# Last two feature blocks of the down projection with tokens stationary, and the final norm over rows

## The chip, the cores and the metric

The kernel runs on one core of one Trainium2 chip. The metric is the device time of one execution in microseconds (us). Five engines matter here: TensorE with its matmuls (PE in the profile) and its weight loads (PEld, a row of its own), VectorE (DVE), ScalarE (ACT), GpSimd (POOL) and the sync engine (SP), whose queue issues the DMAs. A matmul multiplies a stationary operand of 128 x up to 128, which a weight load brings in first, with a moving operand of 128 x N, and adds the product to an accumulator bank (PSUM) of 512 fp32 columns.

## The reference

One inference step of a two-layer decoder trunk over 256 prompt tokens and 64 sample tokens (T = 320 in all), D = 1024 features, fp32. Each layer is a mixer (spatial gating in layer 0, mLSTM in layer 1) and a gated MLP; every sub-layer has an RMS norm ahead and a residual add behind. What matters here is the end of the second layer:

```python
def conv_ffn(x, buf, w_up, conv_w, conv_b, w_down):
    up = x @ w_up
    a, g = jnp.split(up, 2, axis=-1)
    a_c, new_buf = causal_dwconv(a, buf, conv_w, conv_b)
    y = (jax.nn.gelu(a_c) * g) @ w_down
    return y, new_buf
...
x = x + y
return (rmsnorm(x, final_norm_g), ...)
# rmsnorm: x * rsqrt(mean(x*x over 1024 features) + EPS) * g
```

`w_down` is 2816 x 1024: 22 blocks of 128 on the contracted side (`KF`) and 8 blocks of 128 on the feature side (`KD`).

## The kernel before, in words

**Layout.** The activations are kept transposed: `xT[:, m, :]` holds feature block m (128 features on partitions) of all 320 tokens. Weights are stationary, tokens move. For fp32 accuracy each operand is split into a high part (`wh`, `yh`) and a low part (`wl`, `yl`), and each product is three matmuls: wh by yh, wh by yl, wl by yh (`chunk`, line 154). So one feature block of the last down projection is 22 x 3 = 66 matmuls of 128 x 320, accumulated in one bank `pm`.

**Weights.** `weights` (line 63) writes the list of all weight chunks in the order of their use; a chunk is up to 8 blocks of 128 x 128 (512 KB). `prefetch` (line 109) loads chunk i + 4 into one of four `raw` buffers through SP, and splits chunk i + 1 (`AHEAD`, `SPLIT_AHEAD`): ScalarE casts the high part (line 136), VectorE subtracts to get the low part (line 137), into one of three buffers. A down block is three chunks, of 8, 7 and 7 blocks. `take` (line 146) hands out the next chunk.

**Order.** The matmuls are pinned to the order of the program; a scheduler places the other engines' instructions.

**The end.** `ffn(1, None)` (line 448) makes 22 blocks of the gated hidden layer (`conv`, `gate`) and calls `final` (line 514). There, for each of the 8 feature blocks m: 66 matmuls into `pm`; three transposes of the block before into row banks `pyt` (tokens on partitions; `to_rows`, line 519); VectorE adds `pm` to `xT` (line 272); ScalarE squares the sum (line 192), and VectorE adds the squares up in `acc` (line 194); ScalarE multiplies by the norm vector, one value per partition (`xg`, line 536). After block 7: six matmuls against a matrix of ones sum the squares over the partitions (line 543), three transposes bring the last block into rows, VectorE turns the sums into means (line 545), GpSimd raises them to -1/2 (line 547), and ScalarE and VectorE scale one half each of the rows of three token tiles (two of 128 tokens, one of 64; lines 551, 552), which SP writes out, 512, 512 and 256 KB (line 553).

Of the kernel before, what the change touches and what calls it, by code (L numbers as in the profile page):

```python
# [16 lines left out]
P = 128  # L17
EPS = 1e-6
TINY = 1e-37
TP = 256  # L20
# [18 lines left out]
class Net:  # L39
# [23 lines left out]
    def weights(self):  # L63
# [42 lines left out]
    AHEAD, SPLIT_AHEAD = 4, 1  # L106
    EARLY_OUT = {(4, 5): (0, 1), (5, 3): (2,), (5, 5): (3, 4), (6, 3): (5,), (6, 5): (6, 7)}

    def prefetch(self, n, m):

        nc = self.nc
        while len(self.loaded) < min(n, len(self.wq)):
            w, b, k0, kn = self.wq[len(self.loaded)]
            raw = self.wraw.tile([P, 8, P], F32, tag="raw", name="raw")
            if w is self.I["a_wv"]:
                kn *= 4
                nc.sync.dma_start(raw[:, :kn, :], w[b, :, 4 * k0:4 * k0 + kn, :])
            else:
                nc.sync.dma_start(raw[:, :kn, :], w[b, :, k0:k0 + kn, :])
            self.loaded.append(raw)  # L120
        while len(self.halved) < min(m, len(self.wq)):
            i = len(self.halved)
            raw, kn = self.loaded[i], self.wq[i][3]
            if self.wq[i][0] is self.I["a_wv"]:
                kn *= 4
# [12 lines left out]
            self.halved.append((wh, wl))  # L138
# [45 lines left out]
    def square_block(self, m, keep=False):  # L184
# [5 lines left out]
        else:  # L190
            self.sq = self.tp.tile([P, T], F32, tag="sq", name="sq", bufs=2)
            nc.scalar.activation(self.sq, x, AF.Square)
            if not keep:
                nc.vector.tensor_tensor(self.acc, self.acc, self.sq, op=ADD)
# [253 lines left out]
    def ffn(self, l, gnext):  # L448
# [3 lines left out]
        with tc.tile_pool(name=f"yf{l}", bufs=1) as yp, tc.tile_pool(name=f"lf{l}", bufs=1) as lp:  # L452
            yh = yp.tile([P, KF, T], F32R, name=f"yh_f{l}")
# [31 lines left out]
            def gate(b, ps):  # L485
# [4 lines left out]
                self.split(yh[:, b, :], yl[:, b, :], y)  # L490
# [16 lines left out]
            rhs = lambda k: (yh[:, k, :], yl[:, k, :])  # L507
# [3 lines left out]
            else:  # L511
                self.final(lambda m: self.block(KF, rhs), lp)

    def final(self, block, lp):

        nc, O = self.nc, self.O
        pts = {}

        def to_rows(m, xg):
# [5 lines left out]
            for t in range(3):  # L525
                self.tr(pts[q][t][:, c * P:(c + 1) * P], self.tokens(xg, t), self.ident)

        prev = None
# [8 lines left out]
        pc = self.psm.tile([P, 512], F32, tag="pm", name="pc")  # L537
        pv = pc[:, 0:6].rearrange("p (t e) -> p t e", e=2)
        rc = self.tp.tile([P, 3], F32, tag="rc", name="rcf", bufs=2)
        ms = self.tp.tile([P, 3], F32, tag="ms", name="msf", bufs=2)  # L540
# [4 lines left out]
        nc.vector.tensor_scalar(ms, pv[:, :, 0], 1.0 / D, EPS, op0=MULT, op1=ADD)  # L545
        for t in range(3):
            nc.gpsimd.tensor_tensor(rc[:, t:t + 1], ms[:, t:t + 1], self.mhalf, op=ALU.pow)
        for t in range(3):
            ps, n = (slice(0, P), P) if t < 2 else (slice(64, P), 64)
            y = lp.tile([P, D], F32, tag="yo", name="yo", bufs=3)  # L550
            nc.scalar.activation(y[ps, 512:], pts[1][t][ps], AF.Copy, scale=rc[ps, t:t + 1])
            nc.vector.tensor_scalar(y[ps, :512], pts[0][t][ps], rc[ps, t:t + 1], None, op0=MULT)
            nc.sync.dma_start(O["y"][t * P:t * P + n, :], y[ps])
# [513 lines left out]
def _lay_out(i):  # L1067
# [20 lines left out]
    a["f_dn"] = np.stack([_blocks(i["f_w_down"][l]) for l in range(2)])  # L1088
    a["f_state"] = np.ascontiguousarray(i["state_ffn_conv"].reshape(2, 16, KF, P).transpose(0, 3, 2, 1))
# [73 lines left out]
```

## Time and profile before

| | us |
|---|---|
| three runs, median (lowest to highest) | 964.74 (964.19 to 965.17) |
| the profiled execution, its own time | 964.48 |
| its span, from the first to the last instruction | 962.8 |
| PE busy in the span | 948.8 |
| start of the last matmul of feature block 7 | 952.65 |

The profiled execution is 1.7 us longer than its span, and 0.26 us below the median of the runs. In the rows of a timeline the first column is the start in us from the span's start and the second the duration in us; then come engine, line, operation, written tile <- read tiles, shapes, and the count. In rows of the stage table the columns are the stretch, its length, the busy time of PE, PEld, DVE, ACT and POOL (with the count of instructions), the granted clock of PE as a share, the share of the DMA engines' time in use, and GB/s. In rows that group instructions, the two numbers after the bar are the busy time in us and the mean of one in ns, then the idle time before them.

### The profile page before, as it was taken

Reading aid. Unit: us, or ns where it says so; the run is one execution under the profiler, and the core shown is the slowest. Engines: PE = TensorE matmul, PEld = TensorE weight load, DVE = VectorE, ACT = ScalarE, POOL = GpSimd, SP = SyncE. Lnnn points to the kernel's source line nnn. Section 1 sums busy time; section 2 is a strip of 40 time slices with the busy share of each in tenths; the row PEclk is TensorE's granted clock in tenths of the full one; section 3 lists DMA queues with packets and bytes.
Section 4 is the critical chain, followed back from the end, with each engine's and each line's share of the span. In section 5 each row is a group of like instructions: output and inputs, shape, how many; then the busy total and the mean of one; then the engine's idle time right before and its main releaser. Section 6 shows DMA issues by size and latency. Waiting matters only on the chain.

```text
span 962.8 us, 17155 instructions
## 1 busy us (share of the span) xinstructions
PE 948.8 (99%) x6529; PEld 923.7 (96%) x6529; DVE 672.1 (70%) x1229; ACT 520.4 (54%) x948; POOL 79.5 (8%) x251
## 2 busy tenths in 40 slices
PE   9999999999999999999999999999999999999996
PEld 7779999999999999999899999999999999999996
DVE  5758985577777764549888877676787777775442
ACT  6557444355544543347777776575665555444332
POOL 2200000010000000013211001010101000000000
PEclk9999999999999999999999999999999999999998
DMA  7836344444444454456566555634473444445531
GB/s 252 237 131 183 125 139 150 148 142 154 153 141 152 145 153 151 148 196 209 192 203 203 178 174 187 209 127 152 87 247 136 154 154 150 139 147 153 155 121 55
DMA packets 57560, 154.71 MB, mean 161 GB/s; under 512 B 7734, under 2 KB 19382, under 8 KB 57478
## 3 DMA queue, kind: packets, MB, share of 16 engines
q1 hardware_dynamic: 57478, 153.62, 49.2%
q8 instruction: 51, 0.84, 0.3%
q14 instruction: 31, 0.25, 0.1%
HBM read 141.66 MB, written 11.94 MB: 160 GB/s over the span
## 4 chain that ended last, share of the span: by engine, by line
PE 85%; issue 10%; DVE 2%; DMA 1%; ACT 0%; SPq 0%; POOL 0%; DVEq 0%; POOLq 0%; ACTq 0%
PE pm L48 74%; PE pv L48 3%; PE num L48 2%; DMA raw<-in_a_wv 1%; PE pvs L48 1%; PE pmix L48 1%; DVE wl L137 1%; PE pCp L48 1%; PE psc L48 1%; PE pcs L48 1%; PE pv L51 1%; PE phn L51 0%; PE pk L51 0%; PE pc L48 0%; PE pg L48 0%
## 5 line engine op out<-in xcount | busy, mean ns | idle before, releaser
L136 ACT CAST wh<-raw 128x1024 fp32r<-128x1024 f32 (+3 forms) x255 | 257.9, 1012 | 306.5 <-PE pm L48 167.1
L137 DVE TENSOR_TENSOR wl<-raw,wh 128x1024 fp32r<-128x1024 f32 (+3 forms) x255 | 301.2, 1181 | 137.8 <-ACT wh L136 135.0
L48 PE MATMUL pm<-xh,wh 128*128 128x320 f32 x1216 | 379.7, 312 | 0.0
L48 PE MATMUL pm<-xh,wl 128*128 128x320 f32 x1216 | 376.0, 309 | 0.0
L48 PE MATMUL pm<-xl,wh 128*128 128x320 f32 x1216 | 375.8, 309 | 0.0
L48 PEld LDWEIGHTS pm<-xh,wh 128*128 128x128 f32 x1216 | 228.5, 188 | 0.7
L48 PEld LDWEIGHTS pm<-xl,wh 128*128 128x128 f32 x1216 | 228.5, 188 | 0.2
L48 PEld LDWEIGHTS pm<-xh,wl 128*128 128x128 f32 x1216 | 228.3, 188 | 0.0
L48 PE MATMUL pm<-yh_f,wh 128*128 128x320 f32 x352 | 109.2, 310 | 0.0
L48 PE MATMUL pm<-yh_f,wl 128*128 128x320 f32 x352 | 108.7, 309 | 0.0
L48 PE MATMUL pm<-yl_f,wh 128*128 128x320 f32 x352 | 108.7, 309 | 0.0
L48 PEld LDWEIGHTS pm<-yl_f,wh 128*128 128x128 f32 x352 | 66.1, 188 | 0.0
L48 PEld LDWEIGHTS pm<-yh_f,wh 128*128 128x128 f32 x352 | 66.1, 188 | 0.0
L48 PEld LDWEIGHTS pm<-yh_f,wl 128*128 128x128 f32 x352 | 66.1, 188 | 0.0
L478 DVE SCALAR_TENSOR_TENSOR fcv<-fpad,vecs,fcv 128x336 f32<-128x336 f32 x88 | 49.5, 565 | 2.2 <-ACT fcv L476 0.7
L272 DVE TENSOR_TENSOR xT<-pm,xT 128x320 f32<-128x320 f32 x40 | 19.6, 490 | 42.8 <-PE pm L48 42.8
L48 PE MATMUL pm<-yhb,wh 128*128 128x320 f32 x128 | 40.2, 314 | 0.0
L48 PE MATMUL pm<-yhb,wl 128*128 128x320 f32 x128 | 39.5, 309 | 0.5 <-DVE wl L137 0.5
L48 PE MATMUL pm<-yh_a,wh 128*128 128x320 f32 x128 | 39.6, 309 | 0.0
L48 PE MATMUL pm<-yl_a,wh 128*128 128x320 f32 x128 | 39.5, 309 | 0.0
L48 PE MATMUL pm<-yh_a,wl 128*128 128x320 f32 x128 | 39.5, 309 | 0.0
L48 PE MATMUL pm<-ylb,wh 128*128 128x320 f32 x128 | 39.5, 309 | 0.0
(254 smaller groups left out, 1273.7 us busy)
## 6 DMA issues: line engine op xcount, KB each, us to landing
raw<-in_f_up SPq DMA_DIRECT2D x88, 512.0 KB, 3.3
raw<-in_b_win SPq DMA_DIRECT2D x48, 512.0 KB, 4.4
raw<-in_f_dn SPq DMA_DIRECT2D x32, 448.0 KB, 3.2
C<-in_C SPq DMA_DIRECT2D x32, 258.0 KB, 4.9
raw<-in_a_win SPq DMA_DIRECT2D x16, 512.0 KB, 3.3
raw<-in_a_wo SPq DMA_DIRECT2D x16, 512.0 KB, 3.6
raw<-in_f_dn SPq DMA_DIRECT2D x16, 512.0 KB, 3.5
out_Cs<-C SPq DMA_DIRECT2D x32, 256.0 KB, 4.2
```

The lines of the kernel that those rows point to most:

```text
L48: self.pin(self.nc.tensor.matmul(out, lhsT, rhs, start=start, stop=stop))
L51: self.pin(self.nc.tensor.transpose(out, in_, ident))
L136: self.last_split = nc.scalar.copy(wh[:, :kn, :], raw[:, :kn, :])
L137: self.last_low = nc.vector.tensor_tensor(wl[:, :kn, :], raw[:, :kn, :], wh[:, :kn, :].bitcast(F32), op=SUB)
L272: self.nc.vector.tensor_tensor(x, ps[:, :T], x, op=ADD)
L478: nc.vector.scalar_tensor_tensor(cv, pd[:, i:i + NC], self.vec(w + i * KF), cv, op0=MULT, op1=ADD)
```

## The change

Feature blocks 0 to 5 stay as they are, without their squares and without the multiplication by the norm vector. The last two (256 features) are computed the other way round: the tokens `yh`, `yl` are stationary and the weights move, 256 columns at a time, so that the result arrives in rows. It is done tile by tile, in the order tile 0 (128 tokens), tile 2 (the 64 sample tokens), tile 1 (128 tokens), all 22 contracted blocks for each (`own`). The residual's last two blocks get into the bank by two transposes ahead of the matmuls (line 604 of the changed kernel). For the sample tile `yh` gets 64 more columns that hold `yl` (a copy on GpSimd in `gate`), so that one matmul makes the high and the low product on the two halves of the partitions, and two matmuls do the work of three.

The weights of these two blocks are needed three times. Of the 22 contracted blocks, ten are loaded and split during feature blocks 2, 3 and 4 (`KEEP`) and stay in the memory of `xh` and `xl`, which is free by then (`room`); the last twelve stay in the three split buffers. `SPLIT_AHEAD` becomes 2. The norm vector is loaded once as a row and spread over all partitions (`gB`, 512 KB).

The norm works on rows: `early` squares and sums the first 768 features of each tile on ScalarE straight out of the transposed rows (`accum_out`), and multiplies them by the norm vector, during tile 0's matmuls. `leave` does the last 256 features of a tile: a square with its sum, the power of -1/2 on GpSimd, the scaling of the first half on ScalarE, of the rest on VectorE, and two DMAs. For tiles 1 and 2 the early sum is put in as a 257th column, so that no addition is needed.

```diff
@@ weights
-            for b in range(KD):
+            k0 = 0
+            for b in range(KD - 2 * l):
                 add(I["f_dn"][l], b, 8, 7, 7)
+                if l and b in self.KEEP:
+                    add(I["f_dnl"], 0, self.KEEP[b], k0=k0)
+                    k0 += self.KEEP[b]
+            if l:
+                add(I["f_dnl"], 0, 4, 4, 4, k0=k0)
...
+    KEEP = {2: 4, 3: 4, 4: 2}
...
@@ prefetch
-            wh = self.wsp.tile([P, 8, P], F32R, tag="wh", name="wh")
-            wl = self.wsp.tile([P, 8, P], F32R, tag="wl", name="wl")
+            if w is self.I["f_dnl"] and k0 < 10:
+                wh, wl = self.room(k0, kn)
+            else:
+                wh = self.wsp.tile([P, 8, P], F32R, tag="wh", name="wh")
+                wl = self.wsp.tile([P, 8, P], F32R, tag="wl", name="wl")
...
@@ gate
-                self.split(yh[:, b, :], yl[:, b, :], y)
+                self.split(yh[:, b, :T], yl[:, b, :], y)
+                if ext:
+                    nc.gpsimd.tensor_copy(yh[:, b, T:], yl[:, b, TP:])
...
@@ final
+        gB = lp.tile([P, D], F32, name="gB_f")
+        nc.sync.dma_start(gB, I["gfin"].to_broadcast([P, D]))
+        self.SPLIT_AHEAD = 2
...
-        for m in range(KD):
+        for m in range(ML):
             ps = block(m)
-            if prev is not None:
-                to_rows(m - 1, prev)
+            if m in self.KEEP:
+                keep()
+            if m > 0:
+                to_rows(m - 1)
             self.residual(m, ps)
-            self.square_block(m, keep=m == KD - 1)
-            prev = lp.tile([P, T], F32, tag="cv", name="xg", bufs=3)
-            nc.scalar.activation(prev, self.xT[:, m, :], AF.Copy, scale=self.vec(V_FIN + m))
...
-        for a, z in ((self.acc, False), (self.sq, True)):
-            for t in range(3):
-                self.mm(pv[:, t, :], self.tokens(a, t), self.ones[:, :2], not z and t == 0, z and t == 2)
-        to_rows(KD - 1, prev)
-        nc.vector.tensor_scalar(ms, pv[:, :, 0], 1.0 / D, EPS, op0=MULT, op1=ADD)
...
+        def early(t):
...
+            for q, n in ((0, 512), (1, 256)):
+                z = pts[q][t][r, :n]
+                nc.scalar.activation(sq[r, :n], z, AF.Square, scale=1.0 / 32, accum_out=ss[r, t, q:q + 1])
+                nc.vector.tensor_tensor(y[:, 512 * q:512 * q + n], z, gB[r, 512 * q:512 * q + n], op=MULT)
...
+        def own(k, t):
...
+            if first:
+                for e in range(2):
+                    x = xz[:, e, :] if t == 2 else self.tokens(self.xT[:, ML + e, :], t)
+                    self.pin(nc.tensor.matmul(a[:, e * P:(e + 1) * P], x, self.ident, start=e == 0, stop=False,
+                                              is_transpose=True))
+            if t < 2:
+                xh, xl = self.tokens(yh[:, k, :T], t), self.tokens(yl[:, k, :], t)
+                self.mm(a, xh, wh, False, False)
+                self.mm(a, xl, wh, False, False)
+                self.mm(a, xh, wl, False, last)
+            else:
+                xs = yh[:, k, TP:TP + P]
+                self.mm(a[:64], xs[:, :64], wl, False, False)
+                self.mm(a, xs, wh, False, last)
+
+        def leave(t):
...
+            nc.scalar.activation(sq[r, :a.shape[-1]], a, AF.Square, scale=1.0 / 32, accum_out=u)
...
+            nc.gpsimd.tensor_tensor(c, u, self.mhalf[r], op=ALU.pow)
+            out = O["y"][t * P:t * P + n, :]
+            nc.scalar.activation(y[:, :512], y[:, :512], AF.Copy, scale=c)
+            nc.sync.dma_start(out[:, :512], y[:, :512])
+            nc.vector.scalar_tensor_tensor(y[:, 768:], a, c, gB[r, 768:], op0=MULT, op1=MULT)
+            nc.vector.tensor_scalar(y[:, 512:768], y[:, 512:768], c, None, op0=MULT)
+            (nc.scalar if t == 1 else nc.sync).dma_start(out[:, 512:], y[:, 512:])
...
+        for t in (0, 2, 1):
+            for k in range(KF):
+                if k == len(rows):
+                    keep()
+                own(k, t)
+                if (t, k) == (0, 3):
+                    to_rows(ML - 1)
+                    for u in (0, 2, 1):
+                        early(u)
+            leave(t)
```

The scheduler's order, at three places. First PE where feature block 5 ends. Before, three transposes of block 4 and then block 6, 128 x 320 at a time (yh_f, yl_f move):

```order
L48 MATMUL pm<-yh_f_8523,wl 128x320
L51 MATMUL pyt<-ident,xg 128x128 x3
L48 MATMUL pm<-yh_f_8523,wh 128x320
L48 MATMUL pm<-yl_f_8524,wh 128x320
L48 MATMUL pm<-yh_f_8523,wl 128x320
```

Now (line numbers of the changed kernel; py_10870 is the bank of tile 0, pyt_10862 a row bank of tile 2, and `xh` here the memory that holds the kept weights):

```order
L48 MATMUL pm<-yh_f_8523,wl 128x320
L51 MATMUL pyt<-ident,xT 128x128 x2
L51 MATMUL pyt_10862<-ident,xT 128x128
L604 MATMUL py_10870<-ident,xT 128x128 x2
L48 MATMUL py_10870<-xh,yh_f_8523 128x256
L48 MATMUL py_10870<-xh,yl_f_8524 128x256
L48 MATMUL py_10870<-xh,yh_f_8523 128x256 x2
```

Two transposes of the residual follow the three of block 4, and the matmuls are 256 columns wide. Second, the casts of the last weight chunks on ACT against the squares of `early`, in the changed kernel, from the middle of feature block 5 on (wh <- raw is a cast, sq_f an early square):

```order
L156 CAST wh<-raw 128x896 [waits DMAHW0_49,DVE_49,PE_49]
L586 ACTIVATE sq_f,ssf<-pyt 128x512 [waits PE_49]
L156 CAST wh<-raw 128x1024 [waits DMAHW1_49,DVE_49,PE_49]
L156 CAST wh<-raw 128x1024 [waits DMAHW2_49,DVE_49,PE_49]
L156 CAST wh<-raw 128x1024 [waits DMAHW3_49,DVE_49,PE_49]
L586 ACTIVATE sq_f,ssf<-pyt 128x256 [waits PE_49,Activation_49]
L586 ACTIVATE sq_f,ssf<-pyt 64x512 [waits Activation_49]
```

The casts of the three last chunks stand ahead of all early squares but one. Third, the end of ACT's queue. Before, from the casts of block 7's chunks on (sq is line 192's square, yo an output row):

```order
L136 CAST wh<-raw 128x896 [waits DMAHW2_49,DVE_49,PE_49]
L192 ACTIVATE sq<-xT 128x320 [waits DVE_49]
L536 ACTIVATE xg<-xT,vecs 128x320
L192 ACTIVATE sq<-xT 128x320 [waits DVE_49,Activation_49]
L536 ACTIVATE xg<-xT,vecs 128x320
L551 ACTIVATE yo<-pyt,rcf 128x512 [waits PE_49,Pool_49] x2
L551 ACTIVATE yo<-pyt_10845,rcf 64x512 [waits PE_49,Pool_49]
```

Now, from tile 0's `leave` on (py_10870, vs_f and pyt are what is squared for tiles 0, 2 and 1):

```order
L626 ACTIVATE sq_f,msf<-py_10870 128x256 [waits PE_49,Activation_49]
L632 ACTIVATE yo<-yo,rcf 128x512 [waits Pool_49]
L621 COPY vs_f<-pyt_10862 64x256 [waits DVE_49,PE_49]
L626 ACTIVATE sq_f,msf<-vs_f 64x257 [waits DVE_49]
L632 ACTIVATE yo<-yo,rcf 64x512 [waits Pool_49]
L626 ACTIVATE sq_f,msf<-pyt 128x257 [waits PE_49,Activation_49]
L632 ACTIVATE yo<-yo,rcf 128x512 [waits Pool_49]
L636 DMA out_y<-yo 128x512 [waits DVE_49]
```

Three scalings after the last matmul have become one, behind one square, and the last DMA is issued by ACT.

More of the change, by code (lines that the diff above doesn't have):

```diff
@@ L452, in ffn @@
         with tc.tile_pool(name=f"yf{l}", bufs=1) as yp, tc.tile_pool(name=f"lf{l}", bufs=1) as lp:
-            yh = yp.tile([P, KF, T], F32R, name=f"yh_f{l}")
+            ext = 0 if gnext is not None else 64
+            yh = yp.tile([P, KF, T + ext], F32R, name=f"yh_f{l}")
             yl = yp.tile([P, KF, T], F32R, name=f"yl_f{l}")
@@ L525, in to_rows, with keep @@
             for t in range(3):
-                self.tr(pts[q][t][:, c * P:(c + 1) * P], self.tokens(xg, t), self.ident)
-        prev = None
-        for m in range(KD):
+                self.tr(pts[q][t][:, c * P:(c + 1) * P], self.tokens(self.xT[:, m, :], t), self.ident)
+        def keep():
+            (wh, wl), kn = self.take()
+            wh, wl = [x[:, :2 * kn, :].rearrange("p (k e) c -> p k (e c)", e=2) for x in (wh, wl)]
+            rows.extend((wh[:, k, :], wl[:, k, :]) for k in range(kn))
@@ L546, in final @@
[L546 to L553, printed above, removed]
+        rc = self.tp.tile([P, 3], F32, tag="rc", name="rcf", bufs=2)
@@ new lines, in own @@
+        def own(k, t):
+            a = banks[t][:, TP:]
+            wh, wl = rows[k]
+            first, last = k == 0, k == KF - 1
+            if first:
[12 more added lines that the diff above has]
+                self.mm(a, xs, wh, False, last)
@@ L556, in layer_b @@
+        banks = [self.psm.tile([P, 512], F32, tag="pm", name="py0")] + pts[1][1:]
+        vs = lp.tile([P, TP + 1], F32, name="vs_f")[64:]
+        for t in (0, 2, 1):
[8 more added lines that the diff above has]
+            leave(t)
     def layer_b(self):
```

75 lines of the change are left out of this document (55 added, 20 removed).

## The prediction

> **What bounds the kernel now.** I read the engines' totals first, then the stages at the end, then single instructions there.
>
> ```profile
> span 962.8 us, 17155 instructions
> PE 948.8 (99%) x6529; PEld 923.7 (96%) x6529; DVE 672.1 (70%) x1229; ACT 520.4 (54%) x948; POOL 79.5 (8%) x251
> ```
>
> PE is busy for 948.8 of 962.8 us, so whatever PE does in the changed blocks counts in full, and so does the time at the end in which it does nothing. The stage table, for a stretch in the middle of the down projection and for the end (columns: stretch, length, PE, PEld, DVE, ACT, POOL, clock, DMA share, GB/s):
>
> ```profile
> 900.00:910.00 10.00, 10.00 (x71) 10.00 (x71) 4.30 (x5) 3.75 (x6) 0.00 (x0) 1.00 0.48 144
> ```
>
> ```profile
> 952.60:957.40 4.80, 2.47 (x21) 2.13 (x19) 2.21 (x5) 2.49 (x5) 1.60 (x3) 0.83 0.00 0
> 957.40:959.40 2.00, 0.00 (x0) 0.00 (x0) 0.61 (x1) 0.38 (x1) 0.00 (x0) 0.50 0.97 391
> 959.40:961.30 1.90, 0.00 (x0) 0.00 (x0) 0.00 (x0) 0.00 (x0) 0.00 (x0) 0.50 1.00 278
> 961.30:962.80 1.50, 0.00 (x0) 0.00 (x0) 0.00 (x0) 0.00 (x0) 0.00 (x0) 0.50 0.01 0
> ```
>
> In the blocks PE is full at clock 1.00, with VectorE and ScalarE at 43 and 38%. At the end there are 4.8 us of norm, 3.9 us of output at 391 and then 278 GB/s, and 1.5 us after the last packet. The change trades one for the other: more on PE, a shorter end.
>
> **PE, what is added.** The steps, from start to start, stand in the timeline around block 7 (three transposes, then its 66 matmuls):
>
> ```profile
> 942.64 0.31 PE L48 MATMUL pm<-yh_f,wl 128*128 128x320 f32 x1
> 942.78 0.49 PE L51 MATMUL pyt<-ident,xg 128*128 128x128 f32 x3
> 943.03 0.39 PE L48 MATMUL pm<-yh_f,wh 128*128 128x320 f32 x1
> 943.26 0.31 PE L48 MATMUL pm<-yl_f,wh 128*128 128x320 f32 x1
> ...
> 952.65 0.32 PE L48 MATMUL pm<-yh_f,wl 128*128 128x320 f32 x1
> ```
>
> From the second matmul (943.26) to the 66th (952.65) are 64 steps in 9.39 us: 0.1467 us for 320 columns. From 942.64 to 943.26 stand two such steps and three transposes: 0.62 - 0.29 = 0.33, so 0.11 a transpose. No row has 256 columns in a long series; the nearest is a series of 258 in the mLSTM layer, each with its own weight load too:
>
> ```profile
> 466.15 0.28 PE L48 MATMUL num<-vh,Ps 128*128 128x258 f32 x1
> ...
> 468.08 0.28 PE L48 MATMUL pCp<-vh,kgl 128*128 128x258 f32 x1
> ```
>
> These are the first and last of 17, 16 steps in 1.93 us: 0.1206. On the line through both widths, 256 columns take 0.1198. Bounds: 0.1174 if time went purely by columns (0.8 x 0.1467), 0.1206 from the row; a far bound, 0.1467, is a rival below.
>
> Before, the last two blocks are 2 x 66 = 132 steps: 132 x 0.1467 = 19.4 us. Now tiles 0 and 1 take 66 each and tile 2 takes 44, 176 in all: 176 x 0.1198 = 21.1 (20.7 to 21.2). So **+1.7** (1.3 to 1.9). The sample tile is the reason: 64 tokens cost two thirds of a full tile. Transposes between the end of block 5 and the last matmul: 6 before (blocks 4 and 5), 12 now (blocks 4 and 5, and six that bring in the residual): 6 x 0.11 = **+0.7** (0.5 if three take the 0.25 us between 942.78 and 943.03). Together the last matmul starts 2.4 us later (1.8 to 2.6): 955.05 instead of 952.65.
>
> A rule for the same step stands in the Trainium skill, "TensorE: Matmul & The Clock Gate", Back-to-back issue gap: warm, N / 2.4 + 2.5 ns. That is 109 ns for 256 columns and 136 for 320; by it PE would add 176 x 0.109 - 132 x 0.136 + 0.7 = 1.9 us, and the sum would come out 0.5 us better than mine. The trace disagrees with it at 320 columns (146.7), so I go by the rows.
>
> **The end, what is removed.** What follows the last matmul:
>
> ```profile
> 953.00 0.49 DVE L272 TENSOR_TENSOR xT<-pm,xT 128x320 f32<-128x320 f32 x1 [7.70 <-PE pm L48]
> 953.58 0.47 ACT L192 ACTIVATE sq<-xT 128x320 f32<-128x320 f32 x1 [8.98 <-DVE xT L272]
> 954.11 0.83 PE L48 MATMUL pc<-ones,sq 128*128 128x2 f32 x6 [0.25 <-ACT sq L192]
> 954.98 0.16 DVE L545 TENSOR_SCALAR msf<-pc 128x3 f32<-128x3 f32 x1 [1.49 <-PE pc L48]
> 955.22 1.60 POOL L547 TENSOR_TENSOR rcf<-msf,mhalf 128x1 f32<-128x1 f32 x3 [87.81 <-DVE msf L545]
> 955.81 1.97 ACT L551 ACTIVATE yo<-pyt,rcf 128x512 f32<-128x512 f32 x3 [1.30 <-POOL rcf L547]
> 955.81 2.20 DVE L552 TENSOR_SCALAR yo<-pyt,rcf 128x512 f32<-128x512 f32 x3 [0.67 <-POOL rcf L547]
> 956.63 1.95 SPq L553 DMA_DIRECT2D out_y<-yo  x3
> ```
>
> Residual add, square, sums on PE, mean, power, scaling, output: from the last matmul's start to the end of the span 962.8 - 952.65 = 10.1 us. Of this chain the change keeps a square, a power, one scaling and a DMA, and 512 KB of the 1280 KB of output; tiles 0 and 2 end under the matmuls that follow them (66 + 44 and 66 steps, 13 and 8 us, longer than the whole end that I work out next). Durations for the new pieces:
>
> ```profile
> L716 ACT COPY vTb<-pm 128x256 f32<-128x256 f32 x16 | 5.9, 368 | 0.0
> L848 ACT ACTIVATE dn<-num 128x1 f32<-128x1 f32 x24 | 4.2, 175 | 7.4 <-DVE bstat L846 7.4
> L551 ACT ACTIVATE yo<-pyt,rcf 128x512 f32<-128x512 f32 x2 | 1.3, 683 | 1.3 <-POOL rcf L547 1.3
> ```
>
> ```profile
> L414 DVE SCALAR_TENSOR_TENSOR y_a<-pmix,vecs,b 128x256 f32<-128x256 f32 x16 | 7.7, 480 | 0.8
> L243 DVE TENSOR_SCALAR dg<-ident,rc 128x128 f32<-128x128 f32 x8 | 1.9, 284 | 3.8 <-POOL rc L221 3.8
> L552 DVE TENSOR_SCALAR yo<-pyt,rcf 128x512 f32<-128x512 f32 x2 | 1.4, 747 | 0.7 <-POOL rcf L547 0.7
> ```
>
> From the last matmul's start:
> - 0.35 until the reader starts (952.65 to 953.00);
> - the square of 128 x 257 with its sum. No row has a sum beside an activation. At least 0.37 (a copy of 256 columns out of the bank), at most 0.47 + 0.18 = 0.65 (the square of 320 above, and a second instruction of one column); I take the small row and the second instruction, 0.55;
> - the power: from the end of its input, 955.14, to the scaling's start, 955.81: 0.67;
> - VectorE, 256 columns with the norm row (0.48) and 256 more scaled: between 0.28 (128 columns) and 0.75 (512), nearer the former, 0.40. Together 0.88; ScalarE's 512 columns beside it are shorter, 0.70;
> - 0.07 to the issue of a DMA (first rows ready 955.81 + 0.75, issue 956.63). ACT issues the last one: no row shows a DMA issued there, so 0 to 0.5 us more; I take 0, as ACT has nothing left to do;
> - ScalarE's half is issued at 0.35 + 0.55 + 0.67 + 0.70 + 0.07 = 2.35, VectorE's at 2.5. 0.8 us pass until the packets run (956.63 to 957.4), then 512 KB at 391 to 278 GB/s, 1.3 to 1.9 us; I take 1.6. Last packet at 4.75;
> - 1.5 us after the last packet.
>
> That is 6.2 us (5.8 with all lower ends, 7.7 with all upper ones) against 10.1: **-3.9** (-4.3 to -2.4).
>
> **What I cost at nothing.** The squares, additions and multiplications by the norm vector of blocks 0 to 5 go from engines that are at 43 and 38%: no gain. Three of the blocks get a fourth weight chunk: a load of up to 512 KB (54 GB/s more on 144, while the page shows up to 252 elsewhere) and one cast and one subtraction more, about 1.2 us each on engines with 5 us to spare in 10; PE would have to wait if one came late, and each chunk is loaded four ahead. The last chunk's cast must wait for block 5's last matmul, since it takes the buffer of block 5's last chunk; cast and subtraction, 2.4 us, are over long before PE reaches its weights, 18 x 3 matmuls and eight transposes (7 us) later, as the order puts all but one early square behind it. Should the early squares stand ahead of it, their 3 to 4 us would use up that cover. The 22 copies on GpSimd (0.35 us each for such a shape) go to an engine with 8% load, and nobody needs them before tile 2; behind them wait the state copies of the next block, which have a block's time to spare. The norm row's DMA, 512 KB, goes through SP once, without a wait, ahead of layer 1's up projection, whose loads run four chunks (14 us) ahead.
>
> **Sum.** 964.48 of the profiled execution + 2.4 - 3.9 = 963.0; the median of the runs lies 0.26 above that execution: **963.2**. With the ends of the bounds: -4.3 + 1.8 = -2.5 to -2.4 + 2.6 = +0.2, so 962.2 to 964.9.
>
> **Rivals.**
> 1. *The weight load sets the step, not the columns.* The profile's row gives a load 188 ns, more than the 120 I want between matmuls:
>
> ```profile
> L48 PEld LDWEIGHTS pm<-yh_f,wl 128*128 128x128 f32 x352 | 66.1, 188 | 0.0
> ```
>
> If a long series of new weights at 256 columns kept the step of 0.1467, the 176 would take 25.8 us, 4.7 more than in my sum: 963.2 + 4.7 = 967.9, slower. At a step of 0.128 gain and loss are equal, from 0.139 on it is slower by over 0.2%. For it: only short series at that width. Against: the 17 steps of 0.1206 had loads too, so loads overlap. The Trainium skill, "TensorE: Matmul & The Clock Gate", LDWEIGHTS, has P / 1.2, 107 ns for 128 columns; the trace's 188 is another number, but by the page too the load would hide under my step. Chance 0.13.
> 2. *The end is shorter still*: the sum costs nothing, the second half of the columns goes at the short row's rate, and the output at 391 GB/s: -2.4 or so, 962.3. For it: a 198 KB output that had no company landed in 2.0 us, where 512 KB of y took 2.6.
>
> ```profile
> out_f_state<-fns SPq DMA_DIRECT2D x2, 198.0 KB, 2.0
> out_y<-yo SPq DMA_DIRECT2D x2, 512.0 KB, 2.6
> ```
>
>    A step purely by columns, 0.1174, points the same way: 176 x 0.0024 = 0.4 us less, 962.8. Chance 0.20, of which 0.03 for that step alone. The formula of the skill's page above would end near it, at 962.7.
> 3. *The end does not get shorter by what the change removes*: a dear sum, ACT's first DMA late, the shorter rows of the output at 278 GB/s. That is the upper end, 964.9, no change. For it: the last 1.9 us of output ran at that rate. Chance 0.14.
>
> **How the numbers follow.** My forecast, 963.2 with its own range 962.5 to 964.0, has 0.53. The bound of 0.2% is 1.93 us, about what a measurement of this kernel can tell from no change; from 964.74 it lies at 962.8, inside the forecast, and I put 0.14 of its 0.53 below. Faster: 0.14 + 0.20 = 0.34. Same: 0.39 + 0.14 = 0.53. Slower: 0.13. The range runs from 962.0 to 965.6: it takes in rivals 2 and 3 and leaves out rival 1 and a little on the low side.
>
> **What would show it.** In the profile after: the steps of the matmuls into the three tiles' banks (0.120; 0.14 or more is rival 1); no wait of PE between block 5 and the last matmul, which starts at about 955.05; the square with its sum (0.55); the time from the last matmul's start to the end (6.2); two outputs of 256 KB at the very end, one on ACT. I would be wrong above all if PE waited for kept weights in blocks 2 to 5, which no term of the sum holds.

## The result, and the profile after

The changed kernel takes 962.71 us (median of 13 runs, 962.04 to 963.65); the kernel before, run beside it, 964.65 us (13 runs, 963.95 to 965.66). The ratio is 0.998, with a 95% interval of 0.9971 to 0.9988: 1.9 us faster, by the interval 1.2 to 2.8. The forecast was 963.2. The profiled execution of the changed kernel took 963.01 us.

The totals of its page:

```profile
span 961.2 us, 17253 instructions
PE 948.7 (99%) x6561; PEld 923.4 (96%) x6561; DVE 672.8 (70%) x1236; ACT 519.4 (54%) x951; POOL 85.9 (9%) x277
```

PE is busy for 0.1 us less than before, although it has 32 matmuls more: the matmuls overlap, so their busy time says nothing here, and the starts have to be read. First the kernel before, at a matmul of its first layer and at the last matmul of feature block 5, then the same two of the changed kernel and its last matmul:

```profile
25.11 0.40 PE L48 MATMUL pv<-wh,xh 128*128 128x512 f32 x1
...
932.63 0.31 PE L48 MATMUL pm<-yh_f,wl 128*128 128x320 f32 x1
```

```profile
25.41 0.40 PE L48 MATMUL pv<-wh,xh 128*128 128x512 f32 x1
...
933.03 0.31 PE L48 MATMUL pm<-yh_f,wl 128*128 128x320 f32 x1
...
947.57 0.28 PE L48 MATMUL pyt<-xh,yl_f 128*128 128x256 f32 x1
...
955.11 0.28 PE L48 MATMUL pyt<-wl,yh_f 128*128 128x256 f32 x1
```

Up to the end of block 5 both programs give PE the same work. Of the 0.40 us by which block 5 ends later, 0.30 is there at 25 us already, in the start-up, and 0.10 comes in the 907 us between. Neither is the change's. From there on it is: 932.63 to 952.65 was 20.02 us, 933.03 to 955.11 is 22.08, so **PE takes 2.06 us more**. From 947.57, the second matmul of tile 1, to 955.11, the 66th, are 64 steps in 7.54 us: 0.1178 each.

The stages (columns as in the stage table of before), two in the changed blocks and four of the end:

```profile
933.00:943.00 10.00, 10.00 (x88) 9.99 (x87) 4.98 (x13) 4.54 (x13) 1.28 (x3) 1.00 0.01 2
943.00:953.00 10.00, 10.00 (x88) 10.00 (x87) 1.93 (x5) 2.32 (x5) 0.95 (x2) 1.00 0.23 74
955.10:957.50 2.40, 0.29 (x3) 0.08 (x1) 0.69 (x2) 1.28 (x3) 0.55 (x1) 1.00 0.00 0
957.50:958.30 0.80, 0.00 (x0) 0.00 (x0) 0.06 (x1) 0.03 (x1) 0.00 (x0) 1.00 0.00 0
958.30:959.80 1.50, 0.00 (x0) 0.00 (x0) 0.00 (x0) 0.00 (x0) 0.00 (x0) 0.62 0.91 350
959.80:961.20 1.40, 0.00 (x0) 0.00 (x0) 0.00 (x0) 0.00 (x0) 0.00 (x0) 0.50 0.00 0
```

PE has no hole in the changed blocks, and VectorE and ScalarE are busy for half of the time at most beside it. After the last matmul come 2.45 us of norm up to the first issue, 0.84 until the output's packets run, 1.44 of packets and 1.39 to the end (by the packets' own times, which the rows' bounds follow roughly). Tiles 0 and 2 have left by then: the second halves of their rows are issued 10.5 and 4.3 us ahead of the last matmul, and tile 2's last packet ends at 953.5.

```profile
944.58 0.42 SPq L636 DMA_DIRECT2D out_y<-yo  x1
950.81 1.29 SPq L636 DMA_DIRECT2D out_y<-yo  x1
```

The norm of tile 1 in single instructions:

```profile
955.49 0.39 ACT L626 ACTIVATE sq_f<-pyt 128x257 f32<-128x257 f32 x1 [5.24 <-PE pyt L48]
955.88 0.20 ACT L626 ACTIVATION_READ_ACCUMULATOR sq_f<-pyt 128x1 f32 x1
956.23 0.55 POOL L630 TENSOR_TENSOR rcf<-msf,mhalf 128x1 f32<-128x1 f32 x1 [6.74 <-ACT sq_f L626]
956.81 0.48 DVE L634 SCALAR_TENSOR_TENSOR yo<-pyt,rcf,gB_f 128x256 f32<-128x256 f32 x1 [6.53 <-POOL rcf L630]
956.81 0.72 ACT L632 ACTIVATE yo<-yo,rcf 128x512 f32<-128x512 f32 x1 [0.72 <-POOL rcf L630]
957.21 0.35 DVE L635 TENSOR_SCALAR yo<-yo,rcf 128x256 f32<-128x256 f32 x1
957.56 0.34 SPq L633 DMA_DIRECT2D out_y<-yo  x1
957.59 0.38 ACTq L636 DMA_DIRECT2D out_y<-yo  x1
```

From the last matmul to the end of the span were 10.1 us and are 961.2 - 955.1 = 6.1: **4.0 us less**. The account of the two profiled executions: +0.3 start-up, +0.1 between, +2.06 PE, -4.0 end: -1.5, where the rounded spans give -1.6. Without the start-up it is -1.8, and -1.9 without the 0.1 too; the medians differ by 1.9.

The 4.0 us come off in two places. The first output was issued 3.98 us after the last matmul (956.63, in the prediction's lines) and is now issued 2.45 after it (957.56): 1.5 us less. From there to the end of the span were 6.1 us and are 3.7: 2.5 us less, as two of the three outputs have left before.

Because the start differs from run to run, the experiments below are read by two lengths of each trace: from block 5's last matmul to the last matmul ("PE part", 22.08 in the changed kernel), and from there to the end of the span ("end", 6.12 with the span to two places). Their times are given with the kernel before on the same chip.

### The profile page after: what moved, and what is told of

It is laid out like the page before. It is cut to its first block, busy times and chain, and to the rows that moved or that the text cites. A ratio compares the mean times of both kernels' runs of the same rounds, so it can differ in the third digit from the quotient of the medians.

```text
span 961.2 us, 17253 instructions
## 1 busy us (share of the span) xinstructions
PE 948.7 (99%) x6561; PEld 923.4 (96%) x6561; DVE 672.8 (70%) x1236; ACT 519.4 (54%) x951; POOL 85.9 (9%) x277
## 4 chain that ended last, share of the span: by engine, by line
PE 92%; DVE 3%; DMA 1%; ACT 1%; issue 1%; SPq 0%; POOL 0%; POOLq 0%; DVEq 0%; ACTq 0%
PE pm L48 79%; PE pv L48 3%; PE num L48 2%; PE pyt L48 1%; DMA raw<-in_a_wv 1%; PE pvs L48 1%; PE pmix L48 1%; DVE wl L157 1%; PE py L48 1%; PE pCp L48 1%; PE pcs L48 1%; PE psc L48 0%; PE pv L51 0%; DVE bcv L793 0%; PE phn L51 0%
## 5 line engine op out<-in xcount | busy, mean ns | idle before, releaser
L156 ACT CAST wh<-raw 128x1024 fp32r<-128x1024 f32 (+3 forms) x252 | 255.3, 1013 | 297.6 <-PE pm L48 166.8
L157 DVE TENSOR_TENSOR wl<-raw,wh 128x1024 fp32r<-128x1024 f32 (+3 forms) x252 | 298.2, 1184 | 130.1 <-ACT wh L156 127.1
L48 PE MATMUL pm<-yh_f,wh 128*128 128x320 f32 x308 | 95.4, 310 | 0.0
L48 PE MATMUL pm<-yl_f,wh 128*128 128x320 f32 x308 | 95.0, 309 | 0.0
L48 PE MATMUL pm<-yh_f,wl 128*128 128x320 f32 x308 | 95.0, 309 | 0.0
L48 PEld LDWEIGHTS pm<-yl_f,wh 128*128 128x128 f32 x308 | 57.8, 188 | 0.0
L48 PEld LDWEIGHTS pm<-yh_f,wh 128*128 128x128 f32 x308 | 57.8, 188 | 0.0
L48 PEld LDWEIGHTS pm<-yh_f,wl 128*128 128x128 f32 x308 | 57.7, 187 | 0.0
```

The source lines that it names most:

```text
L48: self.pin(self.nc.tensor.matmul(out, lhsT, rhs, start=start, stop=stop))
```

## Where the gain comes from: two experiments

**Norm over rows alone.** Feature blocks 6 and 7 as before, the norm as in the change; each tile leaves in two pieces, all through SP.

```diff
-            for b in range(KD - 2 * l):
+            for b in range(KD):
                 add(I["f_dn"][l], b, 8, 7, 7)
...
+        self.chunk(ps, rhs, True, False)
+        to_rows(ML - 1)
+        for u in range(3):
+            early(u)
...
+        self.residual(ML, ps)
+        to_rows(ML)
+        for t in range(3):
+            nc.scalar.activation(sq[r, :P], pts[1][t][r, 384:], AF.Square, scale=1.0 / 32, accum_out=ms[r, t, 2:3])
+            nc.vector.tensor_tensor(ms[r, t, 2:3], ms[r, t, 2:3], ms[r, t, 0:1], op=ADD)
+        for t in range(3):
+            leave(t)
```

(The first chunk is one of block 7.)

> One part of the change alone: the norm over rows (norm vector as a row, squares summed on ScalarE out of transposed rows, here 896 features early, during block 7), with feature blocks 6 and 7 as before, 320 columns at a time. My theory: the end got shorter because tiles 0 and 2 leave under the last tile's matmuls, not because of how the norm is computed. So here the last matmul starts where it stood before (PE adds nothing), and the end, which keeps the residual add, three transposes, a square with its sum (0.45 for 128 columns), an addition, the power, the scalings and all 1280 KB of output, stays near the one of before: 0.35 + 0.5 + 0.45 + 0.45 + 0.3 + 0.7 + 0.75 + 0.85 until packets run, 3.6 of packets, 1.5 after: 9.5 us (9.0 to 10.2) against 10.1; time 964.1, slower than the changed kernel by 1.4. Rival: the norm over rows is what shortened the end, and the stationary tokens only cost 2 us. Then the end falls to 7 us or less here and the time to 961.5, faster than the changed kernel.

Measured: 964.83 us against 964.43, ratio 1.0004 (0.9995 to 1.0013): no gain. The end (the last matmul, the first output's issue and the sixth's):

```profile
953.80 0.31 PE L48 MATMUL pm<-yh_f,wl 128*128 128x320 f32 x1
...
957.22 0.34 SPq L576 DMA_DIRECT2D out_y<-yo  x1
...
960.44 0.54 SPq L579 DMA_DIRECT2D out_y<-yo  x1
```

The span ends at 963.8: an end of 10.0 us, where the kernel before has 10.1. The first output is issued 3.4 us after the last matmul, 0.6 sooner than before, but the sixth one 3.2 us later. One part of the theory failed: PE adds 0.34 us (PE part 20.36), as three more transposes stand ahead of the last matmul here, those of block 6. So in this form the sums on ScalarE and the norm vector as a row gain nothing while all three tiles still have to leave behind the last matmul, and the rival, an end of 7 us or less, falls. A row norm whose outputs are issued sooner was not tried. What the whole change has beyond this run is the order tile by tile, which takes two of three tiles out of the end, and results that arrive in rows, which take the residual add and the last transposes out of it.

**Work off the path taken away.** The kernel before, with less beside PE.

```diff
-            self.square_block(m, keep=m == KD - 1)
-            prev = lp.tile([P, T], F32, tag="cv", name="xg", bufs=3)
-            nc.scalar.activation(prev, self.xT[:, m, :], AF.Copy, scale=self.vec(V_FIN + m))
+            if m in (0, KD - 1):
+                self.square_block(m, keep=m == KD - 1)
+            prev = self.xT[:, m, :]
+            if m >= KD - 2:
+                prev = lp.tile([P, T], F32, tag="cv", name="xg", bufs=3)
+                nc.scalar.activation(prev, self.xT[:, m, :], AF.Copy, scale=self.vec(V_FIN + m))
```

> The kernel before, without the squares and the sums of squares of feature blocks 1 to 6 and without the multiplication by the norm vector in blocks 0 to 5 (that part of the norm is left out). My theory: this work lay beside a PE that was full, and taking it away gives nothing: last matmul at the same place, end 10.1 us, time within 0.3 us of before. Rival: part of the gain of the change came from this work, by casts that come earlier: 0.5 us or more faster than before.

Measured: 964.54 against 964.43, ratio 1.0002 (0.9993 to 1.0011); the last matmul starts at 952.31 in a run that started 0.4 us earlier, and the end is 10.0 us. The removed squares and multiplications were worth nothing, as the prediction had it.

## What the step costs PE: two experiments

**The step by width.** Narrower moving operands in tiles 2 and 1, the same weight loads.

```diff
             if t < 2:
...
+                if t == 1 and not last:
+                    c = 128 if k < 11 else 192
+                    a, wh, wl = a[:, :c], wh[:, :c], wl[:, :c]
...
+                if not last:
+                    c = 64 if k < 11 else 224
+                    a, wh, wl = a[:, :c], wh[:, :c], wl[:, :c]
```

> The changed kernel with narrower matmuls in two tiles (the remaining columns of those products are left out): in tile 2, 64 columns for the first 11 contracted blocks and 224 for the next ten; in tile 1, 128 columns for the first 11 and 192 for the next ten; the weight loads stay as they are. It measures the step by width. Theory by columns: the step of 0.1178 at 256 is columns alone (0.1467 x 0.8 = 0.1174), so 0.103 at 224, 0.088 at 192, 0.059 at 128, 0.029 at 64, and the last matmul starts some 5 us earlier. Theory of a floor: each step needs its own weights, and the transposes of 128 columns take 0.1085; then 192, 128 and 64 columns all take about 0.107 to 0.11, 224 the same, and the last matmul starts only 1.1 us earlier.

Measured: PE part 20.76 us, 1.32 less (the one run: 961.06 us). Rows of tile 2 at 64 and 224 columns, then of tile 1 at 128 and 192 (128*64 is a stationary operand of 64 columns, 128*128 one of 128):

```profile
942.30 0.22 PE L48 MATMUL pyt<-xl,yh_f 128*64 128x64 f32 x1
942.36 0.28 PE L48 MATMUL pyt<-xh,yh_f 128*128 128x64 f32 x1
942.47 0.22 PE L48 MATMUL pyt<-xl,yh_f 128*64 128x64 f32 x1
...
943.66 0.28 PE L48 MATMUL pyt<-wh,yh_f 128*128 128x224 f32 x1
943.78 0.27 PE L48 MATMUL pyt<-wl,yh_f 128*64 128x224 f32 x1
943.88 0.27 PE L48 MATMUL pyt<-wh,yh_f 128*128 128x224 f32 x1
...
945.38 0.27 PE L48 MATMUL pyt<-wh,yh_f 128*128 128x224 f32 x1
...
947.46 0.27 PE L48 MATMUL pyt<-xl,yh_f 128*128 128x128 f32 x1
...
948.46 0.39 PE L48 MATMUL pyt<-xl,yh_f 128*128 128x128 f32 x2
...
949.72 0.27 PE L48 MATMUL pyt<-wh,yl_f 128*128 128x192 f32 x1
...
952.85 0.27 PE L48 MATMUL pyt<-wl,yh_f 128*128 128x192 f32 x1
```

At 192 columns 28 steps take 3.13 us, 0.112 each; at 128, 9 take 1.00, 0.111. The rows at 64 columns show a floor that goes with the stationary operand: behind a matmul with 64 stationary columns the next starts after 0.06, behind one with 128 after 0.11. At 224 columns 16 steps take 1.72 us, but their mean of 0.108 is of two kinds: behind 128 stationary columns the trace has 0.109 to 0.113, the floor again, and behind 64 it has 0.098 to 0.105, which is 0.46 ns a column (0.103). So behind 128 stationary columns the step does not change from 128 to 224, and there the theory of columns falls. At 256 columns the step of 0.1178 is set by columns (0.46 ns each, as in 0.1467 for 320), and the two meet, by an estimate from these numbers, at 0.11 / 0.00046 = 240 columns. So the change's width lies just above the corner. With one feature block instead of two, 128 columns, 132 steps of 0.111 and 22 pairs of 0.17 would take 18.4 us, by an estimate from this run's rows, where 66 steps of 0.1467 took 9.7.

That the floor is the weight load itself is a reading and not shown: the number of stationary columns sets the length of the load (0.14 us for 64 and 0.19 for 128 in the profile, overlapping), but the long step stands behind the matmul with 128 columns and not ahead of it.

The Trainium skill, "TensorE: Matmul & The Clock Gate", LDWEIGHTS, gives a load 1/1.2 ns a column, by estimate 107 ns for 128 and 53 for 64. The floors of 0.11 and 0.06 us lie near these figures, while the profile's 188 ns for a load, which overlaps its neighbours, does not show them. The formula that the prediction tried for its step, from the Trainium skill, "TensorE: Matmul & The Clock Gate", Back-to-back issue gap, gives 109 ns at 256 columns, but that section calls it the gap of an isolated matmul and says that in a stream of loads and matmuls both set the spacing. This stream has 117.8, and the trace decides.

**The residual's transposes.** Taken away (the residual of the last 256 features is left out; the first matmul of each tile then starts its bank).

```diff
-            if first:
-                for e in range(2):
-                    x = xz[:, e, :] if t == 2 else self.tokens(self.xT[:, ML + e, :], t)
-                    self.pin(nc.tensor.matmul(a[:, e * P:(e + 1) * P], x, self.ident, start=e == 0, stop=False,
-                                              is_transpose=True))
```

> The changed kernel without the six transposes that bring the residual's last 256 features into the banks (this part of the residual is left out). Theory: each costs PE 0.11 us, as the floor of a step with its own weights does: the time from block 5's last matmul to the last matmul shrinks by 0.65 us, from 22.1 to 21.4. Rival: they fill gaps that PE has anyway where it passes from one tile to the next; then under 0.2.

Measured (one run, 962.25 us), block 5's last matmul and the last matmul:

```profile
933.00 0.31 PE L48 MATMUL pm<-yh_f,wl 128*128 128x320 f32 x1
...
954.42 0.28 PE L48 MATMUL pyt<-wl,yh_f 128*128 128x256 f32 x1
```

That is 21.42, 0.66 less: 0.11 for each of six, in full.

## The cover of the last weight chunk

The split of the last chunk, put behind the early squares and products (`e_sq` and `e_low` are the last of each); chunks are split one ahead again instead of two:

```diff
-        self.SPLIT_AHEAD = 2
+        self.SPLIT_AHEAD = 1
...
-                if k == len(rows):
+                if k == len(rows) == 14:
+                    with self.tc.issue_after(self.e_sq.ins), self.tc.issue_after(self.e_low.ins):
+                        keep()
+                elif k == len(rows):
                     keep()
```

> The changed kernel with the split of the last weight chunk put behind the early squares and products of all tiles (on ScalarE behind six squares, on VectorE behind their products), instead of ahead of them. PE's first need of this chunk's high part is at 940.42 in the trace of the changed kernel, of its low part at 940.65. The early squares end at 938.7 and the early products at about 940.4, so the cast ends at 939.8 and the subtraction at about 941.6. Theory of the prediction, that the cover of some 7 us is used up: PE waits 0.9 to 1.0 us there, and the last matmul starts that much later: time 963.6. Rival: there is room to spare even then (VectorE and ScalarE are under 50% busy in this stretch), no wait, 962.7.

Measured: 963.40 us against 964.52, ratio 0.9991 (0.9982 to 1.0); PE part 23.20, 1.12 more. The wait:

```profile
940.88 1.23 DVE L157 TENSOR_TENSOR wl<-raw,wh 128x1024 fp32r<-128x1024 f32 x1
...
941.03 0.28 PE L48 MATMUL py<-wh,yl_f 128*128 128x256 f32 x1
942.16 0.39 PE L48 MATMUL py<-wl,yh_f 128*128 128x256 f32 x1 [0.85 <-DVE wl L157]
```

PE starts 1.13 us after its last matmul, not 0.12: it waits for the low part, and this is the only wait of PE behind block 5 in this run. VectorE and ScalarE at 50 and 45% in the stage table did not mean spare time for this chunk. That the scheduler put the split ahead of the early squares is worth about half of what the change gains: 1.1 us by the trace, 0.8 by the gains over the kernel before (1.1 here, 1.9 for the change).

## What the end consists of: four experiments

**Sample tile last.**

```diff
-            (nc.scalar if t == 1 else nc.sync).dma_start(out[:, 512:], y[:, 512:])
+            (nc.scalar if t == 2 else nc.sync).dma_start(out[:, 512:], y[:, 512:])
...
-        for t in (0, 2, 1):
+        for t in (0, 1, 2):
...
-                    for u in (0, 2, 1):
+                    for u in (0, 1, 2):
```

> The changed kernel with the tiles in the order 0, 1, 2: the 64 sample tokens last. PE's sum is the same. At the end 256 KB are written instead of 512, but the sample tile needs a copy and an addition ahead of its square (0.37 + 0.43 and two hops, 0.9 in all). My theory: what is saved on the output is less than its bytes say, since in the kernel before the 64 rows at the end ran at 252 GB/s and below where full tiles ran at 403, so 256 KB take 1.0 to 1.1 us against 1.3 for 512 KB; the end becomes 6.1 + 0.9 - 0.25 = 6.7 us, 0.6 slower than the changed kernel. Rival: bytes count; 256 KB take 0.65, the end is 6.1 + 0.9 - 0.65 = 6.35. Third: the copy and the addition cost nothing, and the end is below 6.0.

Measured: 963.53 us against 964.43, ratio 0.999 (0.9981 to 0.9999); end 7.07 us, 0.95 more than in the changed kernel. The last matmul, the copy and the addition, and two slices of the output; then a slice of the changed kernel's output:

```profile
954.77 0.28 PE L48 MATMUL pyt<-wh,yh_f 128*128 128x256 f32 x1
955.08 0.37 ACT L621 COPY vs_f<-pyt 64x256 f32<-64x256 f32 x1 [3.48 <-PE pyt L48]
955.48 0.43 DVE L622 TENSOR_TENSOR vs_f<-vs_f,pyt 64x256 f32<-64x256 f32 x1 [3.86 <-ACT vs_f L621]
955.94 0.42 ACT L626 ACTIVATE sq_f<-vs_f 64x257 f32<-64x257 f32 x1 [0.49 <-DVE vs_f L622]
```

```profile
959.20:959.60 0.40, 0.00 (x0) 0.00 (x0) 0.00 (x0) 0.00 (x0) 0.00 (x0) 0.50 1.07 236
960.00:960.40 0.40, 0.00 (x0) 0.00 (x0) 0.00 (x0) 0.00 (x0) 0.00 (x0) 0.50 0.76 169
```

```profile
958.80:959.20 0.40, 0.00 (x0) 0.00 (x0) 0.00 (x0) 0.00 (x0) 0.00 (x0) 0.50 1.05 410
```

The square starts 1.17 us after the last matmul instead of 0.38. And the output does not pay it back at all: 256 KB in 64 rows move at 169 to 236 GB/s, 512 KB in 128 rows at 384 to 410, so both take about 1.4 us, and the packets of the 64 rows begin 1.2 us after the first issue instead of 0.8. Of the 0.95, 0.79 stand ahead of the square and 0.16 behind it. My direction held; the size, 0.6, was too small because I still credited 0.25 to the smaller output.

**No second queue.**

```diff
-            (nc.scalar if t == 1 else nc.sync).dma_start(out[:, 512:], y[:, 512:])
+            nc.sync.dma_start(out[:, 512:], y[:, 512:])
```

> The changed kernel with its last output issued by SP instead of ACT, so that SP issues both halves of the last tile. In the trace of the changed kernel SP's issue takes 0.34 us and ACT's begins 0.03 after it at 0.38. My theory: the second queue saves the wait for SP's first issue: with SP alone the second half is issued 0.35 later, but the 16 DMA engines are still busy with the first 256 KB then (0.65 us at 400 GB/s), so only what lies beyond shows: last landing 0 to 0.35 later, I take 0.1; end 6.2 us against 6.1. Rival: ACT's first and only DMA pays for a cold queue (the 0 to 0.5 us of the prediction); then SP alone is as fast or up to 0.3 faster, end 5.8 to 6.1.

Measured: 962.73 us against 964.52, ratio 0.9983 (0.9974 to 0.9992); end 6.12 us, the same as with ACT's queue; the 0.1 that my theory took did not come. SP issues the second half 0.44 us after the first (957.76 and 957.32), where ACT issues it 0.03 after, and that is hidden by the first half's packets: the last packet ends 4.73 us after the last matmul in both. The ACT queue neither costs nor saves here.

**Three pieces.** The first piece leaves early, by halving ScalarE's scaling.

```diff
+            if t == 1:
+                nc.scalar.activation(y[:, :256], y[:, :256], AF.Copy, scale=c)
+                nc.sync.dma_start(out[:, :256], y[:, :256])
+                nc.vector.scalar_tensor_tensor(y[:, 768:], a, c, gB[r, 768:], op0=MULT, op1=MULT)
+                nc.sync.dma_start(out[:, 768:], y[:, 768:])
+                nc.scalar.activation(y[:, 256:512], y[:, 256:512], AF.Copy, scale=c)
+                nc.vector.tensor_scalar(y[:, 512:768], y[:, 512:768], c, None, op0=MULT)
+                nc.scalar.dma_start(out[:, 256:768], y[:, 256:768])
+                return
```

> The changed kernel with the last tile's output in three pieces that leave as they are ready: columns 0 to 255 (ScalarE, SP's queue), 768 to 1023 (VectorE, SP), 256 to 767 (both, ACT's queue). My theory: the end is now bound from the scaling on by issue, 0.85 us to the first packets, 512 KB at 400 GB/s and what follows; the first piece is ready 0.3 us earlier, so packets begin 0.3 earlier and the last one comes 0.2 to 0.3 earlier, less 0.1 for ScalarE's second instruction: end 5.9 us (5.8 to 6.1), time 962.5. Rival: the last issue sets the landing, whatever went before; then the end stays at 6.1 or grows to 6.3, as the last piece is issued 0.05 to 0.1 later.

Measured: 962.40 us against 964.52, ratio 0.9981 (0.9972 to 0.9989), which does not tell it from the changed kernel; but the end is 6.31 us, 0.19 longer. My theory of a shorter end was wrong here. The scaling and the issues, then the stretch behind the last packet:

```profile
956.08 0.51 ACT L633 ACTIVATE yo<-yo,rcf 128x256 f32<-128x256 f32 x1 [0.72 <-POOL rcf L630]
...
956.50 0.49 ACT L637 ACTIVATE yo<-yo,rcf 128x256 f32<-128x256 f32 x1
956.62 0.34 SPq L634 DMA_DIRECT2D out_y<-yo  x1
957.02 0.41 ACTq L639 DMA_DIRECT2D out_y<-yo  x1
957.05 0.38 SPq L636 DMA_DIRECT2D out_y<-yo  x1
```

```profile
959.10:960.69 1.59, 0.00 (x0) 0.00 (x0) 0.00 (x0) 0.00 (x0) 0.00 (x0) 0.50 0.00 0
```

Two halves on ScalarE end 0.91 us after the scaling starts, one whole 0.72, so the last issue comes 0.97 after that start instead of 0.78. The end is longer by the same 0.19, as the rival has it, but the rival's mechanism is not shown. In the run with SP alone the last issue came 0.4 later than in the changed kernel and the end was the same. And here the last packet ends 4.71 us after the last matmul, against 4.73 in the changed kernel: the early piece made up for the later issue. What is longer stands behind the last packet, 1.6 us against 1.4 in the changed kernel. Only one trace has it, and its cause stays open.

**VectorE's order turned round.** An early piece without an instruction more.

```diff
+            if t == 1:
+                nc.vector.tensor_scalar(y[:, 512:768], y[:, 512:768], c, None, op0=MULT)
+                nc.vector.scalar_tensor_tensor(y[:, 768:], a, c, gB[r, 768:], op0=MULT, op1=MULT)
+                nc.scalar.activation(y[:, :512], y[:, :512], AF.Copy, scale=c)
+                nc.sync.dma_start(out[:, 512:768], y[:, 512:768])
+                nc.sync.dma_start(out[:, :512], y[:, :512])
+                nc.scalar.dma_start(out[:, 768:], y[:, 768:])
+                return
```

> The changed kernel with VectorE's two operations on the last tile in the other order (columns 512 to 767 first, which need no norm row, then 768 to 1023), and its output in three pieces: 512 to 767 as soon as it is ready (SP), 0 to 511 behind ScalarE's one instruction (SP), 768 to 1023 (ACT). Unlike in the run with three pieces before, no engine gets an instruction more, so the last issue stays at 0.78 us after the scaling starts, and the first piece is issued 0.4 after it. My theory: packets begin 0.35 earlier, and the last 384 KB take 0.95 us from 0.85 after the last issue, so the last packet comes 0.3 earlier than in the changed kernel; less 0.1 for one more semaphore at the end the end is 5.9 us (5.8 to 6.0). Rival: what follows the last issue is fixed at 3.64 us, as in the changed kernel and in the run with three pieces; then the end is 6.1 to 6.2.

Measured: 962.18 us against 964.62, ratio 0.9976 (0.9967 to 0.9985); end 5.99 us, 0.13 shorter than in the changed kernel.

```profile
955.65 0.35 DVE L633 TENSOR_SCALAR yo<-yo,rcf 128x256 f32<-128x256 f32 x1 [6.53 <-POOL rcf L630]
956.04 0.34 SPq L636 DMA_DIRECT2D out_y<-yo  x1
956.04 0.48 DVE L634 SCALAR_TENSOR_TENSOR yo<-pyt,rcf,gB_f 128x256 f32<-128x256 f32 x1
...
956.56 0.37 ACTq L638 DMA_DIRECT2D out_y<-yo  x1
```

The last issue came 0.91 after the scaling starts, later than I had it (0.78), since VectorE's second operation now starts behind the first where the two overlapped by 0.08 before. The end still got shorter, so what follows the last issue is not fixed: 3.4 us here, 3.64 in the changed kernel, 3.24 with SP alone. This is the best version of the study by the length of its end; by their times the intervals of the two overlap, and the profiled execution's start was 1.1 us earlier than that of the changed kernel.

## Why the prediction was right, point by point

- **The step.** 0.1198 came from the line through the rows at 258 and 320 columns; measured 0.1178, near the lower bound of 0.1174. Over 176 steps that is 0.35 us: +1.37 instead of +1.7. The mechanism held, and this term is the one that was mis-sized most. The step by columns alone (0.1174, with 962.8), which the prediction gave a chance of 0.03, is nearer to what came than its own line. Why the series of 258 is dearer than the line from the origin is open.
- **The transposes.** +0.7 by the sum, 0.66 by the run without them.
- **The end.** 6.2 predicted, 6.1 measured. By terms: to the reader 0.35, measured 0.38; square and sum 0.55, measured 0.60 (0.39 and 0.20: two instructions, as assumed); power 0.67, measured 0.73; VectorE 0.88, measured 0.75, as the second operation is shorter than assumed (0.35) and starts before the first has ended; 2.25 from issue to the last packet, measured 2.25; 1.5 after, measured 1.4. The first three terms were 0.14 too small together and VectorE's 0.13 too large: that they cancel is luck. The 0 to 0.5 us for ACT's first DMA rested on no row; the run without it showed nothing.
- **What was costed at nothing.** The work off the path: 0 by the run without it. The cover of the last chunk: 5.1 us are left in the changed kernel, from the low part's end at 935.5 to its first use at 940.65, and with the split behind the early squares PE waits 1.0 us, as the condition had it. No kept weight came late: from the last matmul of block 1 to that of block 5 the changed kernel takes 40.06 us, the kernel before 40.05.
- **The sum.** -1.5 predicted, -1.9 measured; 0.35 of the difference is the step, the rest the end. The mark of 0.2%, or 1.93 us, that the prediction set between "faster" and "same" lies within 0.01 of the measured 1.94: the runs do not tell which of the two it is.
- **Rival 1**, the load sets the step: not at 256 columns, but it was close. The floor behind 128 stationary columns is 0.11 and the step 0.118; my argument that short series at 258 had loads too was right for 258 and would have failed at 224 with 128 stationary columns, where the step is 0.111 and not 0.103.
- **Rival 2**, the end shorter still: the end did not get shorter than the forecast by more than 0.1; the sum costs its second instruction, and the output's packets took 1.4 us, between the 1.3 of the rival and the 1.6 of the sum.
- **Rival 3**, the slow output: its evidence was misread. The 278 GB/s at the end of the kernel before were not a rate that every output has at the end: the 64-row tile stood last there, and 64 rows ran at 169 to 236 GB/s when they stood last again. In the changed kernel a full tile is last and runs at 384 to 410.

## What to carry to other kernels

When all tiles leave behind the last matmul, a small loss on the bounding engine can buy a large piece of the end, if the work is turned so that the tiles finish one by one; here 2.5 of the 4.0 us gained at the end come from outputs that have left before and 1.5 from a shorter way to the first output, and the norm over rows alone gained nothing. Before the operands are swapped, compare the new moving width with the floor that the stationary columns set (0.11 us for 128 here): 256 columns cost 7% more time in PE's steps here, and 128 columns, by the estimate above, would have nearly doubled one block's time. And what stands behind a full engine is free only with its cover: put behind six squares on ScalarE and their products on VectorE, the same split costs 1 us.

## What the runs showed of the hardware that I had not expected

- A sum beside an activation is an instruction of its own on ScalarE (0.18 to 0.20 us) behind it.
- An output of 64 rows keeps the DMA engines as busy in its first full slice (share 1.07) as one of 128 rows (1.05) at little more than half the rate, 236 against 410 GB/s; later slices fall to a share of 0.76 at 169 GB/s. Whether the count of rows or the partitions they come from (64 to 127 in all these kernels) decide was not tried.
- The start-up moves by nearly as much as the change does, 1.6 us against 1.9: the matmul at 25.11 us in the kernel before starts between 24.27 and 25.86 in the ten other profiled executions, whose program is the same up to there. From it to the last matmul of feature block 1 in the second layer's down projection (892.58 in the kernel before) it is 867.5 to 867.8 in all of them. Differences of some tenths between kernels that differ at the end are therefore better read in the trace, from a common matmul, than in the times.
